# The two MLP products of a decoder layer by seven quarter products in place of eight

## Chip, cores and metric

The kernel runs on one core of a Trainium2 chip. The metric is the device time of one execution in microseconds, the median of the runs.

## What is computed

One decoder layer on 1024 prompt tokens and 64 sample tokens (8 batches of 8), 1088 in all, of width 1024. An attention sub-layer (differential heads and sparse-attention heads, both with caches) is followed by an output projection and a dense MLP with four times the width. Everything is fp32. The part that matters here:

```python
mix = jnp.concatenate([o_diff, o_nsa], axis=-1) @ w_out          # 1088 x 1024 @ 1024 x 1024
x = x + rms_norm(mix, g_post_mix)
hm = rms_norm(x, g_pre_mlp)
ff = jnp.square(jax.nn.relu(hm @ w_up)) @ w_down                 # w_up 1024 x 4096, w_down 4096 x 1024
x = x + rms_norm(ff, g_post_mlp)
```

## The kernel before

An fp32 operand is kept as two tiles of TensorE's fast fp32 type, `hi` (a rounded copy, made on ScalarE) and `lo` (what is left, a subtraction on VectorE or GpSimd). Each product is three products: hi by hi, lo by hi, hi by lo. With weights as the stationary 128x128 operand, the moving operand is a stretch of tokens.

The instructions of a stage are written for each engine in a program order; the scheduler of the framework then orders each engine's queue by when operands are ready in its own model, with the program order as priority, and puts in the semaphores. Buffers of a pool are reused in turn. Pools are stacked in SBUF from the left (and, where `side="right"`, from the right) in the order in which they are opened; a tile of a new pool waits for the accesses to those earlier tiles that lay at its addresses (`reuse_waits="tile"`).

Around the change there are three stages. `stage_diff` is the last attention stage; its pools on the left are `xa` (split input, 70 KB a partition), `b` and `sg`, `sm` (constants, masks, small tiles), `kv2`, `pp2` and others. `phase_out` projects its result (`mixT`, in DRAM) by `w_out`, nine token tiles of two products each (L1267), with `front` (load and split of a tile), `prod`, and `post` (norm, residual stored to `x1d`, second norm, transposes into the split tile `xt`). Its 16 split weight tiles (`w2`) are the first pool on the left, over `xa`.

`phase_mlp` goes over 16 groups of 256 hidden columns and three token chunks (`CHUNKS`, 384, 384, 320). `up` (L1335) makes two blocks of 24 matmuls, `r` and `h` are relu and square, split into hi and lo on ScalarE, GpSimd and VectorE (L1339 to L1343), and stay in SBUF. `down` of the step before (L1355) then makes eight blocks of six matmuls, and VectorE adds each to the accumulator `acc` in SBUF (L1361). The weights of the next group are loaded and split meanwhile (L1231, L133, L162). A chunk needs only its own token tiles, so `up` of the first chunk starts while `phase_out` still works on the last tiles, and `finish` (transposes, norm, residual, store; L1387 to L1404) of a chunk goes beside the matmuls of the next.

## Time and profile before

| what | value |
|---|---|
| median of three runs (lowest, highest) | 1871.66 us (1869.86, 1874.77) |
| span of the profiled execution | 1873.6 us |
| TensorE busy | 1783.9 us, 95% |
| VectorE, ScalarE, GpSimd busy | 961.5, 720.6, 530.2 us |

For the profiled execution only its span is listed, from the first to the last instruction; it lies 1.9 us above the median and within the three runs. A row of a busy-time view gives the line of the kernel, the engine (PE is TensorE's matmuls, PEld its weight loads, DVE VectorE, ACT ScalarE, POOL GpSimd), output and inputs, and the shape. The ends of matmuls are modelled, so pace is read from starts or from long runs of them.

### The profile page before, as it was taken

Reading aid. Unit: us, or ns where it says so; the run is one execution under the profiler, and the core shown is the slowest. Engines: PE = TensorE matmul, PEld = TensorE weight load, DVE = VectorE, ACT = ScalarE, POOL = GpSimd, SP = SyncE. Lnnn points to the kernel's source line nnn. Section 1 sums busy time; section 2 is a strip of 40 time slices with the busy share of each in tenths; the row PEclk is TensorE's granted clock in tenths of the full one; section 3 lists DMA queues with packets and bytes.
Section 4 is the critical chain, followed back from the end, with each engine's and each line's share of the span. In section 5 each row is a group of like instructions: output and inputs, shape, how many; then the busy total and the mean of one; then the engine's idle time right before and its main releaser. Section 6 shows DMA issues by size and latency. Waiting matters only on the chain. (4 is left out here: it accounts for less than half of the span.)

```text
span 1873.6 us, 31247 instructions
## 1 busy us (share of the span) xinstructions
PE 1783.9 (95%) x11379; PEld 1566.2 (84%) x11379; DVE 961.5 (51%) x2519; ACT 720.6 (38%) x1987; POOL 530.2 (28%) x749
## 2 busy tenths in 40 slices
PE   6788999999999999999979999999999999999996
PEld 6777776676657788778868799999999999999996
DVE  4357767667754666666564553333333333333336
ACT  4254446556652455555463342222222222222212
POOL 1133325333321111111151023333333333333313
PEclk8899899999999999999989999999999999999998
DMA  8531000022102524324263331111111111111104
GB/s 169 119 86 44 17 12 21 6 80 52 28 8 58 155 72 125 100 66 124 68 201 106 124 119 46 43 43 45 42 45 45 46 46 46 45 46 46 46 1 169
DMA packets 186533, 129.38 MB, mean 69 GB/s; under 512 B 30115, under 2 KB 177419, under 8 KB 186379
## 3 DMA queue, kind: packets, MB, share of 16 engines
q1 hardware_dynamic: 185082, 125.11, 23.5%
q10 hardware_dynamic: 1296, 2.27, 0.5%
q8 instruction: 90, 1.47, 0.3%
q14 instruction: 65, 0.52, 0.1%
HBM read 102.56 MB, written 24.78 MB: 68 GB/s over the span
## 5 line engine op out<-in xcount | busy, mean ns | idle before, releaser
L1355 PE MATMUL Dn<-h,w 128*128 128x384 f32 (+1 forms) x2304 | 388.6, 327 | 2.1 <-DVE w L1401 2.1
L1335 PE MATMUL U<-xt,w 128*128 128x384 f32 (+1 forms) x2304 | 388.5, 326 | 0.2 <-ACT xt L133 0.2
L1355 PEld LDWEIGHTS Dn<-h,w 128*128 128x128 f32 x2304 | 381.8, 188 | 2.3 <-ACT w L1395 2.3
L1335 PEld LDWEIGHTS U<-xt,w 128*128 128x128 f32 x2304 | 380.4, 188 | 0.6 <-ACT xt L133 0.4
L331 PE MATMUL M<-w,xt 128*128 128x384 f32 (+4 forms) x1584 | 294.6, 331 | 13.5 <-ACT nat L133 13.2
L1361 DVE TENSOR_TENSOR acc<-Dn,acc 128x384 f32<-128x384 f32 (+1 forms) x360 | 191.8, 535 | 204.9 <-PE Dn L1355 203.5
L331 PEld LDWEIGHTS M<-w,xt 128*128 128x128 f32 (+1 forms) x1584 | 245.1, 191 | 28.9 <-ACT nat L133 14.7
L162 POOL TENSOR_TENSOR w<-raw,w 128x512 fp32r<-128x512 f32 x128 | 170.8, 1346 | 177.4 <-ACT w L133 177.4
L421 ACT ACTIVATE p<-S,nm 128x512 f32<-128x512 f32 (+3 forms) x288 | 160.1, 562 | 103.6 <-DVE nm L416 57.1
L133 ACT ACTIVATE w<-raw 128x512 fp32r<-128x512 f32 (+1 forms) x160 | 96.6, 609 | 241.8 <-PE U L1335 166.0
L1343 DVE TENSOR_TENSOR h<-r,h 128x384 fp32r<-128x384 f32 (+1 forms) x96 | 52.0, 542 | 261.8 <-POOL r L1342 261.8
L412 DVE TENSOR_REDUCE nm<-S 128x1 f32<-128x512 f32 (+3 forms) x288 | 148.0, 527 | 58.1 <-PE S L411 37.0
L1339 ACT ACTIVATE r<-U 128x384 f32<-128x384 f32 (+1 forms) x96 | 45.4, 473 | 342.3 <-PE U L1335 342.3
L404 PE MATMUL S<-kst,qs 128*128 128x512 f32 (+3 forms) x576 | 163.2, 376 | 9.0 <-ACT p L421 7.9
L1342 POOL TENSOR_TENSOR r<-r 128x384 f32<-128x384 f32 (+1 forms) x96 | 77.3, 805 | 328.6 <-ACT h L1341 328.6
L475 POOL TENSOR_SCALAR p<-p,coef 128x640 f32<-128x640 f32 (+7 forms) x128 | 92.8, 738 | 146.4 <-DVE coef L472 79.6
L404 PEld LDWEIGHTS S<-kst,qs 128*128 128x128 f32 x576 | 94.5, 196 | 21.7 <-ACT p L421 11.1
L169 POOL TENSOR_TENSOR rs_r<-rs_t,mhalf 128x1 f32<-128x1 f32 (+1 forms) x63 | 36.3, 577 | 249.1 <-DVE rs_t L167 236.0
L1267 PE MATMUL C<-w,mh 128*128 128x512 f32 (+1 forms) x432 | 105.5, 401 | 0.8 <-DVE ctmp L1282 0.8
L351 POOL TENSOR_TENSOR rope<-nat,sin 128x128 f32<-128x128 f32 (+3 forms) x81 | 36.3, 448 | 245.5 <-ACT nat L133 234.4
L1267 PEld LDWEIGHTS C<-w,mh 128*128 128x128 f32 (+1 forms) x432 | 78.4, 184 | 22.3 <-DVE ctmp L1282 1.1
L511 PEld LDWEIGHTS T<-ident,p 128*128 128x128 f32 x528 | 57.1, 141 | 39.3 <-issue 35.6
(265 smaller groups left out, 2395.1 us busy)
## 6 DMA issues: line engine op xcount, KB each, us to landing
kvp<-cache_diff_kv SPq DMA_DIRECT2D x128, 128.0 KB
raw<-w_up SPq DMA_DIRECT2D x64, 256.0 KB
raw<-w_down SPq DMA_DIRECT2D x64, 256.0 KB
raw<-w_in SPq DMA_DIRECT2D x32, 192.0 KB
raw<-w_in SPq DMA_DIRECT2D x40, 128.0 KB
xin<-x_prompt SPq DMA_DIRECT2D x8, 512.0 KB
...
```

Of the source, the lines that this page charges most:

```text
L133: self.nc.scalar.activation(out, in_, AF.Copy, scale=scale)
L162: (nc.vector if self.lo_dve else nc.gpsimd).tensor_sub(lo, raw, f32(hi))
L331: nc.tensor.matmul(ps[1][:m, :n], self.xt[c][:, a, k, c0:c0 + m], ws[k][:, b, :n], start=i == 0, stop=i == len(ops) - 1)
L404: nc.tensor.matmul(S[:, a * P - lo:b * P - lo], qs[:, ps, j, :], kst[hf][:, kc, a * P - lo:b * P - lo], start=ps == 0, stop=ps == 1 and no ...
L412: nc.vector.reduce_max(nm[:, n:n + 1], S[:, a * P - lo:b * P - lo], axis=AX.X, negate=True)
L421: nc.scalar.activation(p[:, a * P:b * P], tiles[n][:, a * P - lo:b * P - lo], AF.Exp, bias=nm[:, 0:1], accum_out=sums[:, n:n + 1])
L475: nc.gpsimd.tensor_scalar(v, v, coef[:, sw + 1, j:j + 1], 0.0, op0=OP.mult, op1=OP.add)
L1267: nc.tensor.matmul(ps[:m], mhs[t][:, a, k, :m], ws[n][k][:, b], start=cnt == 0, stop=cnt == 3 * KC - 1)
L1335: nc.tensor.matmul(U[:, :n], ups[f][k // 4][:, a, k % 4, :], self.xt[c][:, b, k, :], start=cnt == 0, stop=cnt == 3 * KC - 1)
L1342: nc.gpsimd.tensor_mul(r[:, :n], r[:, :n], r[:, :n])
L1355: nc.tensor.matmul(O_[:, :n], dns[dm // 2][:, a, f, (dm % 2) * P:(dm % 2 + 1) * P], hs[f][:, b, :n], start=cnt == 0, stop=cnt == 5)
L1361: nc.vector.tensor_add(acc[c][:, dm], O_[:, :n], acc[c][:, dm])
```

## The change

Both MLP products are cut into 2x2 quarters of the matrices, and each set of eight quarter products is replaced by seven products of sums of quarters (Strassen's scheme in Winograd's form, one level). `left` and `right` make the sums of the weight's and of the token side's quarters, in place, and split each of the seven (`split2`). The tokens are cut into two halves of 544 (`HT`): even and odd tiles, each with half of the sample tokens; a matmul has 272 columns (`QT`).

The MLP becomes two stages. `phase_up` holds all seven factors of the token side in SBUF (`xc`, made by `x_factor` from `xf`, 12 of the 14 pieces after `phase_out`), goes over 16 pairs of hidden blocks, makes the seven factors of the next pair's weights meanwhile, combines the products out of four two-bank accumulators, and stores relu squared to `hT` in DRAM. `phase_down` goes over eight groups of 512 hidden rows, loads weights and `hT` rows, makes seven factors of each two steps ahead (`factor`), and adds every product to one of seven accumulators; in the last group the accumulators are folded into the four quarters (`FOLD`), and `finish` follows for ten token tiles. The pools are stacked anew: `xca` and `ur` now lie to the left of `w2`, `xcb` and `us` take the place of `w2`, `cc` and `cl`, and `sp` takes the place of `xf` on the right.

```diff
+HT = TOK // 2
+QT = HT // 2
+UORD = (0, 5, 1, 6, 4, 3, 2)
+DORD = (0, 6, 4, 5, 1, 3, 2)
+FOLD = {0: ((5, 0), (1, 0)), 4: ((2, 4), (4, 6)), 5: ((6, 5), (3, 6), (2, 5), (4, 5))}
 GELU_C = 2.0 * math.sqrt(2.0 / math.pi)
...
+        self.hT = scratch("hT", [FF, TOK])
...
+        ws = []
+        for k in range(KC):
+            raw = self.rp.tile([P, 4, 256], F32, name="ur", bufs=4).rearrange("p a n -> p (a n)")
+            nc.sync.dma_start(raw, w_out[k * P:(k + 1) * P])
+            w = self.wp.tile([P, 2, D], FR, name="w")
+            for n in range(2):
+                c = slice(n * 512, n * 512 + 512)
+                self.act_copy(w[:, 0, c], raw[:, c])
+                nc.gpsimd.tensor_sub(w[:, 1, c], raw[:, c], f32(w[:, 0, c]))
+            ws.append(w)
...
-            self.transpose_to_xt(tmp, t, self.psT)
+            for hf in range(2):
+                T = self.psT.tile([P, 4, P], F32, name="T", tag="T")
+                for k in range(4):
+                    kk = hf * 4 + k
+                    nc.tensor.transpose(T[:, k, :m], tmp[:m, kk * P:(kk + 1) * P], self.ident[:m, :m])
+                ks = slice(hf * 4, hf * 4 + 4)
+                if t == NT:
+                    for h in range(2):
+                        self.act_copy(self.xf[:, ks, h, HT - 32:HT], T[:, :, h * 32:h * 32 + 32])
+                else:
+                    self.act_copy(self.xf[:, ks, t % 2, t // 2 * P:t // 2 * P + P], T[:, :, :])
...
+            if t == 5:
+                self.x_factor(0, 0)
+                self.x_factor(5, 0)
...
+    def split2(self, w, src, lo):
+        self.act_copy(w[:, 0], src)
+        lo.tensor_sub(w[:, 1], src, f32(w[:, 0]))
+    def right(self, q, i, w, add, lo, first):
+        b11, b12, b21, b22 = q
+        if i == first:
+            add.tensor_sub(b12, b22, b12)
+            add.tensor_add(b11, b11, b12)
+        if i == 4:
+            add.tensor_sub(b12, b22, b11)
+        if i == 3:
+            add.tensor_sub(b21, b21, b11)
+        self.split2(w, {0: b11, 6: b12, 4: b12, 5: b11, 1: b21, 3: b21, 2: b22}[i], lo)
+    def left(self, q, i, w, add, lo, s2=None):
+        a11, a12, a21, a22 = q
+        if i == (6 if s2 is None else 5):
+            add.tensor_sub(a11, a11, a21)
+            add.tensor_add(a21, a21, a22)
+        t = a11 if s2 is None else s2
+        if i == 5:
+            add.tensor_sub(t, a22, a11)
+        if i == 2:
+            add.tensor_sub(a12, a12, t)
+        self.split2(w, {0: a11, 6: a11, 4: a21, 5: t, 1: a12, 3: a22, 2: a12}[i], lo)
+    def x_factor(self, i, p):
+        c = slice(p * QT, (p + 1) * QT)
+        q = [self.xf[:, k * 4:k * 4 + 4, t, c] for k, t in ((0, 0), (0, 1), (1, 0), (1, 1))]
+        self.right(q, i, self.xc[i][:, :, :, c], self.nc.vector, self.nc.gpsimd if i in (1, 6, 2) else self.nc.vector, 5)
+    def phase_up(self, wp, tp, psU, close):
+        nc, A, rp = self.nc, self.A, self.rp
+        w_up = A["w_up"][0]
+        NJ = FF // 256
+        raws, W, S2 = {}, {}, {}
+        def load(j):
+            raws[j] = []
+            for kh in range(2):
+                r = rp.tile([P, 4, 256], F32, name="ur", bufs=4)
+                nc.sync.dma_start(r, w_up[kh * 512:kh * 512 + 512, j * 256:j * 256 + 256]
+                                  .rearrange("(k p) c -> p k c", p=P))
+                raws[j].append(r)
+        def factor(j, i):
+            if j == NJ:
+                return
+            r0, r1 = raws[j]
+            q = (r0[:, :, 0:P], r1[:, :, 0:P], r0[:, :, P:256], r1[:, :, P:256])
+            W[j, i] = w = wp.tile([P, 2, 4, P], FR, name="us", bufs=8)
+            if i == 5:
+                S2[j] = wp.tile([P, 4, P], F32, name="s2", bufs=2)
+            self.left(q, i, w, nc.vector, nc.vector if i in (0, 5) else nc.gpsimd, S2.get(j, 0))
+        def mm(ps, j, i, start, pq):
+            w, x = W[j, i], self.xc[i]
+            for p in pq:
                 cnt = 0
                 for a, b in ((0, 0), (1, 0), (0, 1)):
...
+                    for k in range(4):
+                        nc.tensor.matmul(ps[:, p, :QT], w[:, a, k, :], x[:, b, k, p * QT:(p + 1) * QT],
+                                         start=start and cnt == 0, stop=cnt == 11, skip_group_check=True)
                         cnt += 1
...
+        def products(j, pq, nxt):
+            s = slice(pq[0], pq[-1] + 1)
+            n = len(pq)
+            def ptile(x):
+                if pq[0] == 0:
+                    self.ups[x] = psU.tile([P, 2, 512], F32, name=f"U{x}", tag=f"U{x}")
+                t = self.ups[x]
+                return t, t[:, s, :QT]
+            def stile(x, bufs=2):
+                return self.sp.tile([P, 2, QT], F32, name=x, bufs=bufs)[:, :n]
+            def store(f, t, c, eng):
+                h = stile("uh", 4)
+                if eng is None:
+                    nc.scalar.activation(h, c, AF.Relu)
+                    nc.scalar.activation(h, h, AF.Square)
+                else:
+                    eng.scalar_tensor_tensor(h, c, 0.0, c, op0=OP.max, op1=OP.mult)
+                r = (2 * j + f) * P
+                nc.sync.dma_start(self.hT[r:r + P, t * HT + pq[0] * QT:t * HT + (pq[-1] + 1) * QT],
+                                  h.rearrange("p a n -> p (a n)"))
+            a, av = ptile("a")
+            mm(a, j, 0, True, pq)
+            s1 = stile("s1")
+            self.act_copy(s1, av)
+            nxt(0)
+            b, bv = ptile("b")
+            mm(b, j, 5, True, pq)
+            u2 = stile("u2")
+            nc.vector.tensor_add(u2, bv, s1)
+            mm(a, j, 1, False, pq)
+            store(0, 0, av, None)
+            nxt(5)
+            mm(b, j, 6, False, pq)
+            u3 = stile("u3")
+            nc.vector.tensor_add(u3, bv, s1)
+            nxt(1)
+            c, cv = ptile("c")
+            mm(c, j, 4, True, pq)
+            c22 = stile("c22", 1)
+            nc.vector.tensor_add(c22, cv, u3)
+            store(1, 1, c22, None)
+            nxt(6)
+            d, dv = ptile("d")
+            mm(d, j, 3, True, pq)
+            nc.vector.tensor_add(u3, dv, u3)
+            store(1, 0, u3, nc.vector)
+            nxt(4)
+            mm(c, j, 2, False, pq)
+            nc.vector.tensor_add(u2, cv, u2)
+            store(0, 1, u2, nc.vector)
+            nxt(3)
+            nxt(2)
+        self.ups = {}
+        load(0)
+        load(1)
+        for i in UORD:
+            if i in (0, 5):
+                factor(0, i)
+                self.x_factor(i, 1)
+            else:
+                self.x_factor(i, 0)
+                factor(0, i)
+                self.x_factor(i, 1)
+        close()
+        for j in range(NJ):
+            if j + 2 < NJ:
+                load(j + 2)
+            if j == 0:
+                products(0, (0,), lambda i: None)
+                products(0, (1,), lambda i: factor(1, i))
+            else:
+                products(j, (0, 1), lambda i: factor(j + 1, i))
+    def phase_down(self, ap, rp, fp, psD):
+        nc, A = self.nc, self.A
+        w_dn = A["w_down"][0]
+        acc = {i: ap.tile([P, 4, HT], F32, name=f"acc{i}") for i in DORD}
+        gp = ap.tile([P, D], F32, name="gpm")
+        nc.scalar.dma_start(gp, A["g_post_mlp"].to_broadcast([P, D]))
+        NG = FF // 512
+        raws, F = {}, {}
+        def load(g):
+            rows = slice(g * 512, g * 512 + 512)
+            ws, hs = [], []
+            for e in range(2):
+                w = rp.tile([P, 2, D], F32, name="dw", bufs=4)
+                nc.sync.dma_start(w, w_dn[rows].rearrange("(q e p) c -> e p q c", e=2, p=P)[e])
+                h = rp.tile([P, 2, TOK], F32, name="dh", bufs=4)
+                nc.sync.dma_start(h, self.hT[rows].rearrange("(q e p) c -> e p q c", e=2, p=P)[e])
+                ws.append(w)
                 hs.append(h)
...
+            raws[g] = ((ws[0][:, :, 0:512], ws[1][:, :, 0:512], ws[0][:, :, 512:], ws[1][:, :, 512:]),
+                       (hs[0][:, :, 0:HT], hs[0][:, :, HT:], hs[1][:, :, 0:HT], hs[1][:, :, HT:]))
+        def factor(g, i):
+            if i == 0 and g + 1 < NG:
+                load(g + 1)
+            wq, hq = raws[g]
+            w = fp.tile([P, 2, 2, 512], FR, name="wf", bufs=3)
+            self.left(wq, i, w, nc.gpsimd, nc.gpsimd)
+            h = fp.tile([P, 2, 2, HT], FR, name="hf", bufs=3)
+            self.right(hq, i, h, nc.vector, nc.vector, 6)
+            F[g, i] = (w, h)
+        def product(g, i, db):
+            w, h = F[g, i]
+            ps = psD.tile([P, 2, 512], F32, name="Dn", tag="Dn")
+            for p in range(2):
                 cnt = 0
                 for a, b in ((0, 0), (1, 0), (0, 1)):
...
+                    for q in range(2):
+                        nc.tensor.matmul(ps[:, p, :QT], w[:, a, q, db * P:(db + 1) * P],
+                                         h[:, b, q, p * QT:(p + 1) * QT], start=cnt == 0, stop=cnt == 5)
                         cnt += 1
...
+            d = acc[i][:, db].rearrange("p (a n) -> p a n", a=2)
+            if g == 0:
+                nc.vector.tensor_copy(d, ps[:, :, :QT])
+            else:
+                nc.vector.tensor_add(d, ps[:, :, :QT], d)
+        steps = [(g, i) for g in range(NG) for i in DORD]
+        load(0)
+        for n in range(2):
+            factor(*steps[n])
+        first = list(range(0, NT, 2)) + [NT]
+        for n, (g, i) in enumerate(steps):
+            if n + 2 < len(steps):
+                factor(*steps[n + 2])
+            for db in range(4):
+                product(g, i, db)
+                if n == len(steps) - 1:
+                    self.finish(rp, psD, gp, first[db], (acc[1], acc[3]))
+            if g == NG - 1:
+                for x, y in FOLD.get(i, ()):
+                    for db in range(4):
+                        e = nc.gpsimd if db % 2 else nc.vector
+                        e.tensor_add(acc[x][:, db], acc[x][:, db], acc[y][:, db])
+        self.finish(rp, psD, gp, first[4], (acc[1], acc[3]))
+        for t in list(range(1, NT, 2)) + [NT + 1]:
+            self.finish(rp, psD, gp, t, (acc[2], acc[4]))
+    def finish(self, rp, psD, gp, t, acc):
         nc, A = self.nc, self.A
...
+        m, c0, r0 = (32, HT - 32, SEQ + 32 * (t - NT)) if t >= NT else (P, t // 2 * P, t * P)
+        x1 = rp.tile([P, 2, 512], F32, name="dw", bufs=4)
+        nc.sync.dma_start(x1[:m], self.x1d[r0:r0 + m].rearrange("p (a n) -> p a n", a=2))
+        tmp = rp.tile([P, 2, 512], F32, name="dh", bufs=4)
+        ss = self.fs.tile([P, 1], F32, name="fss", bufs=2)
+        N = psD.tile([P, 2, 512], F32, name="Dn", tag="Dn")
         for hf in range(2):
...
             for i in range(4):
...
+                nc.tensor.transpose(N[:m, hf, i * P:(i + 1) * P], acc[hf][:, i, c0:c0 + m], self.ident)
+        nc.scalar.activation(tmp[:m], N[:m], AF.Square, accum_out=ss[:m])
+        r = self.rstd(self.fs, ss[:m], D, m)
+        nc.vector.scalar_tensor_tensor(tmp[:m], N[:m], r[:m], gp[:m].rearrange("p (a n) -> p a n", a=2),
+                                       op0=OP.mult, op1=OP.mult)
+        nc.gpsimd.tensor_add(tmp[:m], tmp[:m], x1[:m])
+        if t >= NT:
+            dst = A["o_y_s"].rearrange("b s d -> (b s) d")[r0 - SEQ:r0 - SEQ + m]
+        else:
+            dst = A["o_y_p"][0, r0:r0 + m]
+        nc.sync.dma_start(dst, tmp[:m].rearrange("p a n -> p (a n)"))
...
+            with self.pool("xca") as xca, self.pool("ur", 4) as self.rp:
+                self.xc = {i: xca.tile([P, 2, 4, HT], FR, name=f"xc{i}") for i in (0, 5)}
+                right = ExitStack()
+                self.xf = right.enter_context(self.pool("xf", side="right")).tile([P, KC, 2, HT], F32, name="xf")
+                with self.pool("w2", 8) as self.wp, self.pool("cc") as cp, self.pool("cl") as cl, \
+                        self.pool("psC", 3, psum=True) as self.psC, self.pool("psT2", 2, psum=True) as self.psT:
+                with self.pool("xcb") as xcb, self.pool("us") as wp, self.pool("psU", psum=True) as psU:
+                    self.xc.update({i: xcb.tile([P, 2, 4, HT], FR, name=f"xc{i}") for i in (1, 2, 3, 4, 6)})
+                    def close():
+                        right.close()
+                        self.sp = right.enter_context(self.pool("sp", side="right"))
+                    self.phase_up(wp, xcb, psU, close)
+                right.close()
+            with self.pool("acc") as ap, self.pool("rd") as rp, self.pool("fd") as fp, self.pool("fs") as self.fs, \
+                    self.pool("psDn", 4, psum=True) as psD:
+                self.phase_down(ap, rp, fp, psD)
```

## Rows read from the trace of the kernel before

**Rows 1.** The page: busy us, share of the span and instructions of each engine.
```profile
PE 1783.9 (95%) x11379; PEld 1566.2 (84%) x11379; DVE 961.5 (51%) x2519; ACT 720.6 (38%) x1987; POOL 530.2 (28%) x749
```

**Rows 2.** Stretches: span, busy of PE, PEld, DVE, ACT, POOL, granted clock, DMA share, GB/s.
```profile
1058.88:1873.60 814.72, 798.48 (x4828) 789.61 (x4826) 304.26 (x572) 188.72 (x381) 244.08 (x232) 0.99 0.18 55
973.20:992.00 18.80, 18.80 (x89) 15.52 (x89) 5.15 (x12) 8.25 (x20) 8.11 (x8) 0.93 0.32 100
...
1112.00:1837.00 725.00, 725.00 (x4415) 724.95 (x4414) 246.69 (x470) 157.29 (x308) 223.63 (x209) 1.00 0.14 42
1837.00:1873.60 36.60, 21.08 (x137) 20.57 (x135) 25.21 (x50) 7.37 (x24) 12.94 (x14) 0.81 0.56 197
```

**Rows 3.** Groups of TensorE's matmuls by shape: count, busy us, mean ns of one.
```profile
L1335 PE MATMUL U<-xt,w 128*128 128x384 f32 x1536 | 272.1, 334 | 0.0
...
L1335 PE MATMUL U<-xt,w 128*128 128x320 f32 x768 | 116.4, 309 | 0.2 <-ACT xt L133 0.2
...
L331 PE MATMUL M<-w,xt 128*128 128x256 f32 x480 | 74.8, 302 | 11.5 <-ACT nat L133 11.5
```

**Rows 4.** Timeline of TensorE, long runs of one shape: start, us, count at the end.
```profile
179.35 3.32 PE L331 MATMUL M<-w,xt 128*128 128x280 f32 x24
...
414.76 3.08 PE L331 MATMUL M<-w,xt 128*128 128x256 f32 x24
...
1382.58 8.51 PE L1335 MATMUL U<-xt,w 128*128 128x384 f32 x48
...
1399.25 7.19 PE L1335 MATMUL U<-xt,w 128*128 128x320 f32 x48
...
1843.87 2.78 PE L1394 MATMUL Dn<-ident,acc 128*128 128x128 f32 x24
```

**Rows 5.** Timeline of VectorE and GpSimd where instructions of both overlap: start, us.
```profile
1104.10 1.28 DVE L1287 SCALAR_TENSOR_TENSOR ctmp<-cx,rs_r,gpre 64x1024 f32<-64x1024 f32 x1 [0.72 <-POOL rs_r L169]
1104.28 1.79 POOL L1342 TENSOR_TENSOR r<-r 128x384 f32<-128x384 f32 x1 [0.21 <-ACT h L1341]
...
1107.30 0.83 POOL L1342 TENSOR_TENSOR r<-r 128x384 f32<-128x384 f32 x1 [1.24 <-ACT h L1341]
...
1381.73 1.30 POOL L162 TENSOR_TENSOR w<-raw,w 128x512 fp32r<-128x512 f32 x1 [0.45 <-ACT w L133]
1381.90 0.49 DVE L1361 TENSOR_TENSOR acc<-Dn,acc 128x320 f32<-128x320 f32 x1 [0.39 <-PE Dn L1355]
...
1867.82 1.25 POOL L1402 TENSOR_TENSOR w<-w,raw 64x512 f32<-64x512 f32 x1 [0.91 <-issue]
1868.38 1.24 DVE L1402 TENSOR_TENSOR w<-w,raw 64x512 f32<-64x512 f32 x1
```

**Rows 6.** Groups by shape on VectorE, ScalarE and GpSimd from 1000 us on.
```profile
L1361 DVE TENSOR_TENSOR acc<-Dn,acc 128x384 f32<-128x384 f32 x240 | 133.3, 557 | 137.4 <-PE Dn L1355 136.0
...
L1361 DVE TENSOR_TENSOR acc<-Dn,acc 128x320 f32<-128x320 f32 x120 | 58.5, 490 | 67.5 <-PE Dn L1355 67.5
...
L162 DVE TENSOR_TENSOR w<-raw,w 128x512 fp32r<-128x512 f32 x16 | 10.7, 696 | 6.0 <-ACT w L133 5.9
...
L1257 DVE TENSOR_TENSOR mh<-mx,mh 128x1024 fp32r<-128x1024 f32 x5 | 6.1, 1218 | 4.5 <-ACT mh L133 4.5
...
L133 ACT ACTIVATE mh<-mx 128x1024 fp32r<-128x1024 f32 x5 | 5.3, 1052 | 1.1 <-PE C L1267 1.1
...
L162 POOL TENSOR_TENSOR w<-raw,w 128x512 fp32r<-128x512 f32 x112 | 148.0, 1331 | 169.8 <-ACT w L133 169.8
...
L169 POOL TENSOR_TENSOR rs_r<-rs_t,mhalf 128x1 f32<-128x1 f32 x23 | 13.6, 592 | 110.5 <-DVE rs_t L167 110.3
```

**Rows 7.** Timeline at the end of phase_out, and the densest stretch of transfers.
```profile
1087.81 5.75 PE L1267 MATMUL C<-w,mh 128*64 128x512 f32 x24
...
1106.43 3.78 PE L1335 MATMUL U<-xt,w 128*128 128x320 f32 x24 [0.22 <-ACT xt L133]
...
1855.00:1860.00 5.00, 5.00 (x42) 4.92 (x40) 3.15 (x8) 1.58 (x5) 0.96 (x1) 1.00 1.03 388
```

More of the change, by code (lines that the diff above doesn't have):

```diff
@@ L1332, in up @@
                 cnt = 0
                 for a, b in ((0, 0), (1, 0), (0, 1)):
-                    for k in range(KC):
-                        nc.tensor.matmul(U[:, :n], ups[f][k // 4][:, a, k % 4, :], self.xt[c][:, b, k, :],
-                                         start=cnt == 0, stop=cnt == 3 * KC - 1)
+                    for k in range(4):
+                        nc.tensor.matmul(ps[:, p, :QT], w[:, a, k, :], x[:, b, k, p * QT:(p + 1) * QT],
+                                         start=start and cnt == 0, stop=cnt == 11, skip_group_check=True)
@@ L1352, in down @@
                 cnt = 0
                 for a, b in ((0, 0), (1, 0), (0, 1)):
-                    for f in range(2):
-                        nc.tensor.matmul(O_[:, :n], dns[dm // 2][:, a, f, (dm % 2) * P:(dm % 2 + 1) * P],
-                                         hs[f][:, b, :n], start=cnt == 0, stop=cnt == 5)
+                    for q in range(2):
+                        nc.tensor.matmul(ps[:, p, :QT], w[:, a, q, db * P:(db + 1) * P],
+                                         h[:, b, q, p * QT:(p + 1) * QT], start=cnt == 0, stop=cnt == 5)
@@ L1357, in down @@
                         cnt += 1
-                if gr == 0:
-                    nc.vector.tensor_copy(acc[c][:, dm], O_[:, :n])
-                else:
-                    nc.vector.tensor_add(acc[c][:, dm], O_[:, :n], acc[c][:, dm])
-        steps = [(gr, c) for gr in range(NG) for c in range(3)]
-        prev = None
-        for gr, c in steps:
-            if c == 0 and gr + 1 < NG:
-                W[gr + 1] = load(gr + 1)
-                self.lo_dve = False
-            hs = up(gr, c)
-            if prev:
-                down(*prev)
-                if prev[0] == NG - 1:
-                    self.finish_chunk(dp, psD, acc, gp, prev[1])
-            prev = (gr, c, hs)
```

87 lines of the change are left out of this document (1 added, 86 removed).

## The prediction

> **What bounds the kernel now.** First the page [rows 1]: TensorE is busy 95% of the span, the others half or less. Then the busy times by stretch [rows 2]: from 1112 to 1837 us, the MLP proper, TensorE is busy 725.00 of 725.00 us at a granted clock of 1.00, VectorE a third, GpSimd 31%. From 1058.88 us (the end of `phase_out`) to the end TensorE stands still for only 814.72 - 798.48 = 16.2 us, nearly all of it in the last 36.6 us. So the MLP is worth what its matmuls cost, every join is covered by other matmuls, and whatever leaves TensorE idle is lost in full.
>
> **TensorE's share of the change.** Before: 3072 matmuls of 384 and 1536 of 320 columns (up [rows 3], and as many in down). Pace from long runs, less the last one's mean duration: (8.51 - 0.334)/47 = 174 ns and (7.19 - 0.309)/47 = 146.4 ns [rows 3, 4]. That is 534.5 + 224.9 = 759.4 us. After: up 16 x 7 x 24 and down 8 x 7 x 48, 5376 of 272 columns. This width does not occur. The line through 320 and 384 gives 125.7 ns; the runs of 256 and 280 columns, (3.08 - 0.302)/23 = 120.8 and (3.32 - 0.30)/23 = 131.3 ns [rows 3, 4], give 127.8. I take 126 (same kind of dense stream): 677.4 us, **-82**; with 127.8 it is -72.
>
> Does the weight load hold up a matmul of 126 ns? PEld is busy 724.95 of 725.00 us [rows 2], but the 256-column runs load 128x128 weights for each matmul at 120.8 ns and the transposes reach (2.78 - 0.272)/23, some 109 ns [rows 3, 4]. So it does not, in my view. The Trainium skill (Perfetto Trace Analysis, Identifying the Most-Contended Engine) says to judge TensorE by the busy share of its weight loads and not by its matmuls. By that the loads would be the bound already; it is the fourth rival below.
>
> **The price list.** PSUM to SBUF adds are 490 and 557 ns for 320 and 384 columns [rows 6], so 0.72 us for 544. VectorE with two SBUF operands: 0.70 us for 512, 1.22 for 1024 [rows 6], so 1.29 for 1088 and 0.74 for 544. GpSimd: 1.33 us for 512 [rows 6]; for 1024 twice that is 2.66, less some fixed part 2.5; for 1088 2.65, for 544 1.41. ScalarE: 1.05 us for 1024.
>
> VectorE and GpSimd are not independent. GpSimd's 384-wide product takes 0.83 us alone, and 1.79 when it starts 0.18 us after a VectorE instruction with two SBUF operands; a VectorE add of 512 takes 1.24 instead of 0.70 and ends 0.55 after the GpSimd add in its way. An add with one operand in PSUM runs through such an overlap at its usual 0.49 [rows 5, 6]. So these times add up when both have work. The Trainium skill (SBUF — State Buffer, Who interferes with whom) gives the rule: VectorE's second SBUF operand and GpSimd go through one exclusive port, and the later one waits. The trace agrees (1.24 and 1.79 us), and without the rule the sum below would be some 40 us lower; it speaks against this change, which moves hundreds of such instructions to these two engines.
>
> **Up, steady state.** A pair of blocks is 168 matmuls, 21.2 us. Port work: GpSimd 5 x 1.33, VectorE (4 sums, 2 lows) x 0.70 and 2 squares x 0.74, 12.3 us. VectorE in all 9.3, ScalarE below 8. The accumulators have one buffer each, but 24 matmuls (3 us) stand between a product and the next into the same one, and the read takes 0.72. Cost nothing; if VectorE came 2 us late, it would show at once.
>
> **Start of phase_out, +8.** Today `w2` lies over `xa`, free early; products of `phase_out` fill the last attention head's waits, PE 18.80 of 18.80 us busy [rows 2]. With `xca` and `ur` (51 KB) to its left, `w2` spans some 51 to 115 KB: its tiles from the third or fourth on lie over `b`, `sg` and `kv2`, in use to the last head. Their splits, 10 x 1.33 = 13.3 us on GpSimd, move behind it. Between 0 and 15; I take 8.
>
> **Start of up, +32.** Today the last product of `phase_out` ends at 1087.81 + 5.75 = 1093.56, and up goes on beside the last tile's norm, 12.9 us to its first use at 1106.43 [rows 7]. Afterwards five of seven `xc` lie over `w2`, `cc` and `cl`, so their factors wait for that last product, call it T. Then come on VectorE 12 x 1.29 + 6 x 0.70, on GpSimd 6 x 2.65 + 5 x 1.33: 42 us through one port. `sp` lies over `xf`, so even the first copy `s1` waits for the last `x_factor`. Before it TensorE can do four of seven products of the first pair; after it 72 matmuls are left, 9 us. The pair ends at T + 51 where its work is 21: 30 lost, 2 more for the granted clock, which falls when TensorE stands still (0.81 in the last stretch [rows 2]). From below: if VectorE did not hold the port, GpSimd alone is 22.5, and 10 are lost. From above: if the port work starts with the last tile's norm done, 42.
>
> **Up to down, +20.** `dw` lies over `xc` tiles that the last product reads, so nothing of `w_down` is loaded before. A group is 2.1 MB of weights and 2.2 of `hT`; at the 388 GB/s that the trace reaches [rows 7] 11 us, its first half 5.6. Then split: 1.05 + 2.5 + 1.29; the first product starts at about 10.5 and lasts 6. The second factor needs the second half: three GpSimd and three VectorE instructions, 11.4 us from 11 on, so 6 more idle. With 3 for the clock: 20; 13 if `hT` comes ahead, 32 at half the rate. The store of `hT` and its loads are elsewhere 4.3 MB in 42 us, 100 GB/s, and cost nothing.
>
> **Down, steady state, +10.** A group is 336 matmuls, 42.3 us. GpSimd: 11 x 2.5 = 27.5. VectorE: 11 x 1.29 and 28 x 0.72 = 34.4. Through the port 41.7. GpSimd is busy 65% of the time; a VectorE instruction that meets it waits on average half of 2.5, so 11 x 0.65 x 1.25 = 9, VectorE 43.4, just above TensorE. The four two-bank buffers let TensorE run about three blocks ahead. 1.2 us a group, 10; bounds 0, and 48 if every one of the 11 waits 1.25.
>
> **The end, +24.** In the last group the port has 7 x 2.5 + 7 x 1.29 of factors left, 32 folds (16 x 1.41 + 16 x 0.74), and GpSimd does ten residual adds and powers (2.5 + 0.59 [rows 6]): 92 us, 4 more to the last store, against 42.3 + 80 x 0.109 = 51 of TensorE. 45 idle, and the folds stand ahead of the last factor in program order, so the last product waits too. Today 16 are idle there: +29, less what VectorE does while GpSimd waits: 24. GpSimd alone, 71 us, gives +8; 30 from above.
>
> **Sum.** -82 + 8 + 32 + 20 + 10 + 24 = +12. The sum is against the span of 1873.6; the median is 1.9 lower: 1871.7 + 12 = **1884 us**, slightly slower. All bounds low: -82 + 0 + 10 + 13 + 0 + 8 = -51; all high: -72 + 15 + 42 + 32 + 48 + 30 = +95.
>
> **Rivals.** (1) Faster: the port costs less than it adds up to, because the two engines' waits fall into each other's gaps at the start of up. If GpSimd alone sets that join (10 in place of 32) and the end (8 in place of 24), the sum is -26; with down at 0 and the other joins as low as they go, -51. 1835 on average. It decides from the point at which the start of up costs less than 14. For it: VectorE and GpSimd are idle half the time today; against it: [rows 5]. (2) Down becomes bound by VectorE behind GpSimd: +48 in place of 10, 1922. For it: 43.4 against 42.3 leaves no reserve; against: the buffers. (3) The joins hide one another so that gain and loss are equal, 1868 to 1876. (4) The weight loads set the pace: 759.4/4608 = 165 ns each, 5376 of them 886 us, +126 in place of -82, 2092. For it: PEld without a gap; against: [rows 4].
>
> **Chances.** About 0.3% (6 us) is what a measurement of this kernel can tell from no change. My forecast, slower by 6 to 40 us: 0.44; (2) 0.09; (4) 0.02; (3) 0.13; (1) 0.32. So faster 0.32, same 0.13, slower 0.55. The forecast's own range is 1878 to 1912. The range that leaves out (4), half of (2) and the better fifth of (1) is 1836 to 1924.
>
> **What would show it.** Pace: runs of 272 columns at 126 ns; above 140 it is the weight loads. Start: first C products after 980 us. A hole of about 30 us between the last C and the second pair of up, with VectorE's and GpSimd's two-operand instructions end to end and stretched. A hole of 10 us and one of 6 at the start of down. Down groups of 43 to 44 us. At the end 40 us with GpSimd busy and TensorE idle. I am wrong if those holes are short because factors were made earlier than I think, or if the stretched instructions do not occur.

## Result and the profile after

The changed kernel takes 1913.58 us (median of four runs, 1910.13 to 1917.81) against 1872.16 for the kernel before (four runs): ratio 1.0225, 95% interval 1.0204 to 1.0246. It is slower, as forecast, but by 41 us where 12 were forecast. That lies inside the wide range of the prediction (1836 to 1924) and 2 us above the forecast's own (1878 to 1912).

The page of the kernel after, busy times, beside [rows 1]:

```profile
PE 1725.2 (90%) x12155; PEld 1497.5 (78%) x12155; DVE 1233.4 (65%) x2539; ACT 806.3 (42%) x1976; POOL 746.3 (39%) x733
```

TensorE has 59 us less to do and the span is 37 us longer (1910.7): about 96 us more in which it stands still. The stretches of the kernel after, columns as in [rows 2]; in order: the hole ahead of the first C, start of up, up, start of down with its first group, six further groups, the last group with `finish`, and a part of up:

```profile
972.10:981.54 9.44, 0.02 (x1) 0.00 (x0) 0.02 (x1) 4.84 (x9) 9.44 (x9) 0.50 0.79 243
1090.84:1152.10 61.26, 30.93 (x184) 28.92 (x183) 47.43 (x43) 27.89 (x46) 38.80 (x18) 0.67 0.12 35
1152.10:1468.42 316.32, 316.32 (x2522) 316.10 (x2520) 129.78 (x189) 107.27 (x173) 99.95 (x71) 1.00 0.30 99
1468.42:1533.90 65.48, 48.34 (x338) 46.28 (x337) 54.99 (x44) 18.96 (x19) 46.17 (x16) 0.90 0.55 204
1533.90:1809.40 275.50, 259.15 (x2016) 253.65 (x2017) 263.60 (x234) 88.06 (x85) 194.38 (x66) 1.00 0.23 83
1809.40:1910.70 101.30, 61.41 (x416) 57.54 (x416) 74.20 (x74) 21.49 (x30) 79.81 (x44) 0.81 0.23 78
1180.00:1400.00 220.00, 220.00 (x1755) 220.00 (x1754) 91.71 (x134) 77.27 (x126) 74.17 (x54) 1.00 0.30 101
```

Only up runs without a gap: 220.00/1755 is 125.4 ns a matmul. In down's six groups VectorE is busy 263.60 of 275.50 us and TensorE stands still for 16. Five of the six groups take 46.5 us each from first matmul to first matmul, where 336 x 125.4 ns are 42.1; the sixth takes 43.0. The instructions of these six, by shape (count, busy us, mean ns, idle time before):

```profile
L1519 PE MATMUL Dn<-hf,wf 128*128 128x272 f32 x2016 | 259.2, 289 | 16.4 <-DVE acc L1526 15.7 <-DVE acc L1524 0.2
...
L1331 POOL TENSOR_TENSOR wf<-dw,wf 128x1024 fp32r<-128x1024 f32 x42 | 118.5, 2821 | 79.3 <-ACT wf L139 79.3
L1526 DVE TENSOR_TENSOR acc<-Dn,acc 128x544 f32<-128x544 f32 x165 | 111.9, 713 | 11.6 <-PE Dn L1519 11.5
L1331 DVE TENSOR_TENSOR hf<-dh,hf 128x1088 fp32r<-128x1088 f32 x42 | 94.7, 2254 | 0.0
```

VectorE's subtraction of 1088 columns takes 2254 ns in place of 1.28 us, its addition from PSUM 713, as forecast. The timeline of the worst step of a group, VectorE, then GpSimd, then TensorE:

```profile
1662.42 3.48 DVE L1338 TENSOR_TENSOR dh<-dh 128x1088 f32<-128x1088 f32 x1
1665.82 0.71 DVE L1526 TENSOR_TENSOR acc<-Dn,acc 128x544 f32<-128x544 f32 x1
1666.45 2.83 DVE L1339 TENSOR_TENSOR dh<-dh 128x1088 f32<-128x1088 f32 x1
...
1661.43 3.32 POOL L1350 TENSOR_TENSOR dw<-dw 128x1024 f32<-128x1024 f32 x1
1664.83 3.31 POOL L1351 TENSOR_TENSOR dw<-dw 128x1024 f32<-128x1024 f32 x1
...
1666.59 1.76 PE L1519 MATMUL Dn<-hf,wf 128*128 128x272 f32 x12 [1.30 <-DVE acc L1526]
1669.97 3.30 PE L1519 MATMUL Dn<-hf,wf 128*128 128x272 f32 x24 [1.63 <-DVE acc L1526]
```

The two engines take turns: each VectorE sum ends 1.1 us after the GpSimd sum that it waited for, each GpSimd sum waits for the VectorE one. The addition that frees a PSUM buffer stands behind them, and TensorE waits.

The start of up shows the same on VectorE's timeline; the last row is a sum of the same shape, and GpSimd has no instruction beside it:

```profile
1101.05 3.58 DVE L1343 TENSOR_TENSOR xf<-xf 128x1088 f32<-128x1088 f32 x1 [2.40 <-POOL xc L1331]
1104.56 3.57 DVE L1338 TENSOR_TENSOR xf<-xf 128x1088 f32<-128x1088 f32 x1
...
1118.57 1.28 DVE L1339 TENSOR_TENSOR xf<-xf 128x1088 f32<-128x1088 f32 x1
```

### The profile page after: what moved, and what is told of

The parts are those of the page before. It is cut to its first block, busy times and chain, and to the rows that moved or that the text cites. A ratio compares the mean times of both kernels' runs of the same rounds, so it can differ in the third digit from the quotient of the medians.

```text
span 1910.7 us, 32861 instructions
## 1 busy us (share of the span) xinstructions
PE 1725.2 (90%) x12155; PEld 1497.5 (78%) x12155; DVE 1233.4 (65%) x2539; ACT 806.3 (42%) x1976; POOL 746.3 (39%) x733
## 4 chain that ended last, share of the span: by engine, by line
PE 71%; DVE 13%; issue 3%; DMA 3%; POOL 2%; ACT 2%; SPq 0%; POOLq 0%; ACTq 0%; DVEq 0%
PE M L337 11%; PE Dn L1519 10%; PE C L1272 5%; PE S L410 5%; PE Ua L1395 5%; PE Ub L1395 5%; PE Uc L1395 5%; PE o L502 5%; PE T L517 4%; PE Ud L1395 3%; DVE hf L1331 2%; DVE acc L1526 2%; PE o L614 2%; PE S L1095 1%; DVE dh L1338 1%
## 5 line engine op out<-in xcount | busy, mean ns | idle before, releaser
L1519 PE MATMUL Dn<-hf,wf 128*128 128x272 f32 x2688 | 358.0, 294 | 47.3 <-DVE acc L1526 29.7
L1519 PEld LDWEIGHTS Dn<-hf,wf 128*128 128x128 f32 x2688 | 348.1, 193 | 56.8 <-DVE acc L1526 33.9
L337 PE MATMUL M<-w,xt 128*128 128x384 f32 (+4 forms) x1584 | 293.0, 330 | 13.1 <-ACT nat L139 12.8
L1331 POOL TENSOR_TENSOR wf<-dw,wf 128x1024 fp32r<-128x1024 f32 x56 | 157.7, 2818 | 119.6 <-ACT wf L139 119.6
L1331 POOL TENSOR_TENSOR us<-ur,us 128x512 fp32r<-128x512 f32 x80 | 118.3, 1481 | 211.8 <-ACT us L139 189.2
L1526 DVE TENSOR_TENSOR acc<-Dn,acc 128x544 f32<-128x544 f32 x196 | 132.9, 712 | 15.1 <-PE Dn L1519 14.9
L1331 DVE TENSOR_TENSOR hf<-dh,hf 128x1088 fp32r<-128x1088 f32 x56 | 127.1, 2270 | 8.0 <-ACT hf L139 8.0
L1395 PE MATMUL Ua<-xc,us 128*128 128x272 f32 x768 | 107.1, 292 | 9.9 <-DVE us L1331 8.9
L1395 PE MATMUL Ub<-xc,us 128*128 128x272 f32 x768 | 103.5, 290 | 9.7 <-ACT us L139 9.7
L1395 PE MATMUL Uc<-xc,us 128*128 128x272 f32 x768 | 108.4, 290 | 3.5 <-POOL us L1331 3.2
L1395 PEld LDWEIGHTS Ua<-xc,us 128*128 128x128 f32 x768 | 102.0, 193 | 10.4 <-DVE us L1331 9.2
```

The lines of the kernel that those rows point to most:

```text
L337: nc.tensor.matmul(ps[1][:m, :n], self.xt[c][:, a, k, c0:c0 + m], ws[k][:, b, :n], start=i == 0, stop=i == len(ops) - 1)
L1331: lo.tensor_sub(w[:, 1], src, f32(w[:, 0]))
L1395: nc.tensor.matmul(ps[:, p, :QT], w[:, a, k, :], x[:, b, k, p * QT:(p + 1) * QT], start=start and cnt == 0, stop=cnt == 11, skip_group_che ...
L1519: nc.tensor.matmul(ps[:, p, :QT], w[:, a, q, db * P:(db + 1) * P], h[:, b, q, p * QT:(p + 1) * QT], start=cnt == 0, stop=cnt == 5)
L1526: nc.vector.tensor_add(d, ps[:, :, :QT], d)
```

## The experiments

The theory: TensorE's 85 us are saved, and the instructions that make the quarter sums and low parts give them back, because VectorE's with two SBUF operands and GpSimd's exclude each other (below, "the port"). Rivals: VectorE's own load, waits for addresses at the joins, transfers, the order of the steps. Times are medians; the ratio is to the kernel before, run on the same chip.

**e1, start of up on VectorE alone.**

```diff
-self.nc.gpsimd if i in (1, 6, 2) else self.nc.vector, 5)
+self.nc.vector, 5)
-nc.vector if i in (0, 5) else nc.gpsimd, S2.get(j, 0))
+nc.vector if j == 0 or i in (0, 5) else nc.gpsimd, S2.get(j, 0))
```

> At the start of up every two-operand instruction goes to VectorE: 6 low parts of the token factors and 5 of the first pair's weight factors leave GpSimd. Theory (their times add up, so a GpSimd instruction costs its own longer time): the hole shrinks by 6 x (2.40 - 1.28) + 5 x (1.33 - 0.70), 10 us; the second pair starts at about 1142 us in place of 1152, time 1904. Rival (the engines work side by side, the hole is VectorE's load): VectorE gets 6 x 1.28 + 5 x 0.70, 11 us more, time 1925. Second rival (ScalarE's copies or the norm of the last tile set the hole): no change, 1911 to 1916.

Measured: 1905.83, ratio 1.0178 (1.0152 to 1.0203); the second pair starts at 1142.1. VectorE's groups by shape there:

```profile
L1331 DVE TENSOR_TENSOR xc<-xf,xc 128x1088 fp32r<-128x1088 f32 x12 | 14.9, 1276 | 0.0
L1331 DVE TENSOR_TENSOR us<-ur,us 128x512 fp32r<-128x512 f32 x7 | 4.5, 680 | 0.3 <-ACT us L139 0.3
```

Eleven instructions more on VectorE, and the second pair starts 10 us earlier, as the port theory said; the rival had the other sign. The time fell by 8 us.

**e2, buffers of down where up's tiles come free first.**

```diff
-with self.pool("acc") as ap, self.pool("rd") as rp, self.pool("fd") as fp, ...
+with self.pool("rd") as rp, self.pool("fd") as fp, self.pool("acc") as ap, ...
-for i in (1, 2, 3, 4, 6)})
+for i in (1, 6, 4, 3, 2)})
-nc.sync.dma_start(self.hT[r:r + P,
+(nc.scalar if j == NJ - 1 and (f, t) != (0, 1) else nc.sync).dma_start(self.hT[r:r + P,
```

> The buffers of down lie so that the first group's weights and hT rows fall on tiles that the last pair of up reads first, and three of the last four stores of hT go by ScalarE's queue. Theory (the join is the wait for those addresses): the loads start some 10 us before the end of up, the holes of 9.2 and 2.4 us shrink to some 4 in all, the first group's first steps are not late, time 1900. Rival (the loads wait for hT to be stored, or the first group is slow because of the split work on GpSimd and VectorE): the first hole stays above 7 us or its time comes back later in the group, 1910 to 1914.

Measured: 1912.14, ratio 1.0203 (1.0178 to 1.0228). The first hole falls from 9.2 to 1.6 us, but the first group takes 60.9 us in place of 56.3: the rival. The addresses were one of two waits in a row; behind them stand the factors, again with VectorE held up (its timeline):

```profile
1475.71 2.74 DVE L1420 SCALAR_TENSOR_TENSOR uh<-u 128x544 f32<-128x544 f32 x1
1478.37 3.47 DVE L1331 TENSOR_TENSOR hf<-dh,hf 128x1088 fp32r<-128x1088 f32 x1
```

**e3, no GpSimd work in down's groups.**

```diff
-self.left(wq, i, w, nc.gpsimd, nc.gpsimd)
+a11, a12, a21, a22 = wq
+t = {0: a11, 6: a11, 4: a21, 5: a11, 1: a12, 3: a22, 2: a12}[i]
+self.act_copy(w[:, 0], t)
+self.act_copy(w[:, 1], t)
```

This kernel leaves out the sums of `w_down`'s quarters, and its low parts are copies, so it does not compute the layer; it is there for its time alone.

> Leaves out the sums of w_down's quarters and makes both tiles of a weight factor by ScalarE copies, so that GpSimd has no work in down but folds and finish. Theory (GpSimd's 11 instructions hold VectorE's two-operand ones up): those fall from 2.2 to 3.4 us to 1.28, VectorE to 34 us a group, the group from 46.5 to 42.1 us; with eight groups and a lighter join and end 35 to 50 us less, 1863 to 1878. Rival (VectorE's additions of PSUM, their order or the number of PSUM buffers set the pace): VectorE's two-operand times fall but the group stays at 45 to 46.5 us, 1905 to 1913. Second rival (ScalarE, now at 14 + 7 copies a group, becomes late): the group is longer, over 1913.

Measured: 1872.61, ratio 0.9999 (0.9988 to 1.0011): 41 us less than the changed kernel. Six groups of it, columns as above, and VectorE's subtraction:

```profile
1531.00:1781.90 250.90, 250.90 (x2019) 250.90 (x2018) 193.25 (x234) 126.34 (x126) 0.00 (x0) 1.00 0.27 92
```

```profile
L1331 DVE TENSOR_TENSOR hf<-dh,hf 128x1088 fp32r<-128x1088 f32 x42 | 53.9, 1282 | 0.0
```

TensorE has no gap and a group takes 41.8 us, 4.7 less than the changed kernel's 46.5. PSUM buffers and the additions alone are not the bound.

**e4, e8: the end.** e4 puts all folds on VectorE (`e = nc.vector`); e8 is

```diff
-tmp = rp.tile([P, 2, 512], F32, name="dh", bufs=4)
+tmp = self.fs.tile([P, 2, 512], F32, name="ft", bufs=6)
-nc.gpsimd.tensor_add(tmp[:m], tmp[:m], x1[:m])
+(nc.vector if t % 4 > 1 or t == NT else nc.gpsimd).tensor_add(tmp[:m], tmp[:m], x1[:m])
```

> All 32 folds of the accumulators on VectorE (0.74 us each alone), none on GpSimd (1.41). Theory (folds add up on both engines): 16 x (1.41 - 0.74), 11 us less of that work, of which 6 to 10 show, time 1904 to 1908. Rival (VectorE, which also empties PSUM, is what the end waits for): 16 x 0.74, 12 us more on it, time 1920 to 1925.

> Five of the ten residual adds of finish go to VectorE, and the result tiles get six buffers of their own. Theory (after the last product GpSimd is the bound: 10 x 2.35 + 10 x 0.55, 29 of 35 us): GpSimd 17, VectorE 10 x 1.24 + 5 x 1.28 = 19, and 6 to 10 us less, time 1904 to 1908. Rival (the chain of transposes, square, power and store, and its PSUM buffers): 0 to 2 us.

Measured: e4 1913.63, ratio 1.0221 (1.0195 to 1.0247); e8 1911.08, ratio 1.0212 (1.0185 to 1.0239). Neither time can be told from the changed kernel's, though in the profiles the last group with `finish` takes 97.6 and 95.8 us in place of 101.3. e4 followed neither theory nor rival: VectorE is busy 28.4 us with all 32 folds, and was busy 24.7 with 16 of them beside GpSimd's. e8 came out near its rival, 2 us less.

**e5, the order 0, 1, 6, 4, 5, 3, 2** in `DORD`.

> Down takes its products in the order 0, 1, 6, 4, 5, 3, 2: the second factor of a group then needs no sums, and the heaviest one (three instructions on VectorE, three on GpSimd) comes a step later. Theory A (the sum of the two engines' times over a whole group is too long): the group stays at 46 to 46.5 us, only the start of down gains 4 to 6, time 1908. Theory B (only the peak is too long for the four PSUM buffers, and the peak now falls into slack): the group falls to 43 to 44.5, time 1888 to 1898.

Measured: 1910.64, ratio 1.0202 (1.0173 to 1.0232); five of the groups take 45.7 us where the changed kernel's take 46.5. That is theory A for the most part: the sum over a group is too long, and the peak's share is 0.8 us. The gain of 4 to 6 us at the start of down did not come: from the end of up to the second group it is 64.8 us in place of 65.6.

**e6, the token side's sums in up.** `hT` is stored as seven combinations; the core of it:

```diff
+nc.vector.tensor_sub(h12, h22, h12)
+put(6, h12)
+nc.vector.tensor_add(o5, h11, h12)
+put(5, o5)
+nc.vector.tensor_sub(o4, h22, o5)
+put(4, o4)
+nc.vector.tensor_sub(o3, h21, o5)
+put(3, o3)
...
-self.right(hq, i, h, nc.vector, nc.vector, 6)
+self.split2(h, hq[i], nc.vector)
```

> The four sums of the token side's quarters are made in up, on VectorE, and hT holds seven combinations in place of four quarters (1.75 times the bytes). Theory (GpSimd and VectorE share one port; up has 21.1 - 12.3 us of it free in a pair, down has none): pairs stay at 21.1 us; in down VectorE has 7 x 1.28 + 28 x 0.71 = 28.9 us and at most 11 waits of 1.2, so the group is TensorE's 42; 8 x 4.4 = 35 us less, 2 to 4 more at the join, time 1872 to 1880. Rival (the sums only move the load): pairs grow to 22 us and more, 16 x 1 back, time over 1890. Second rival (transfers, 6 MB in a group, 143 GB/s): the group waits for dh.

Measured: 1886.68, ratio 1.0075 (1.0047 to 1.0103). Pairs stay at 21.1 us, groups fall to 42.4; six of them:

```profile
1537.90:1792.10 254.20, 254.20 (x2018) 254.20 (x2017) 222.29 (x212) 86.69 (x84) 182.20 (x67) 1.00 0.37 121
```

Down's gain came as forecast. The join went wrong: the hole before the first product grew from 9.2 to 18.1 us. The hole as a stretch, and VectorE's timeline in it:

```profile
1475.10:1493.20 18.10, 0.00 (x1) 0.00 (x0) 4.25 (x6) 2.19 (x3) 7.02 (x3) 0.58 0.97 352
```

```profile
1478.89 0.72 DVE L1470 TENSOR_TENSOR uh<-uh 128x544 f32<-128x544 f32 x1
1493.20 3.69 DVE L1331 TENSOR_TENSOR hf<-dh,hf 128x1088 fp32r<-128x1088 f32 x3 [13.60 <-ACT hf L139]
```

VectorE has made the last pair's four sums by 1479.6 us and then stands idle for 13.6, while the DMA engines are 97% busy: by these rows the join waits for transfers, which the seven combinations have made longer (the second rival, but at the join alone). No run tried that apart; in e10, where the loads start earlier, the hole before the first product is 1.1 us.

**e7, `xca` and `ur` at the right end of SBUF** (`side="right"` on both pools).

> xca and ur go to the right end of SBUF, so that w2 lies over xa again, as in the kernel before. Theory (the split of w_out waits for the last head's tiles): GpSimd's 16 low parts come before 970 us, the hole of 9.4 us before the first C shrinks to 1 or 2, time 1904 to 1907. Rival (the hole is the last head's own latency, mixT stored and loaded again): no change, 1911 to 1915.

Measured: 1923.65, ratio 1.0276 (1.0245 to 1.0308), slower than either expected. The splits do come early (from 942.9 us) and the hole is gone, but the last attention matmuls end at 988.8 in place of 972.1. VectorE and GpSimd there, first beside a run of six GpSimd instructions, then beside a run of eight:

```profile
947.35 6.81 DVE L422 TENSOR_TENSOR nm<-nm 128x1 f32<-128x1 f32 x1
...
956.80 0.97 DVE L422 TENSOR_TENSOR nm<-nm 128x1 f32<-128x1 f32 x1
...
946.74 7.41 POOL L1246 TENSOR_TENSOR w<-ur,w 128x512 fp32r<-128x512 f32 x6
...
956.48 10.85 POOL L1246 TENSOR_TENSOR w<-ur,w 128x512 fp32r<-128x512 f32 x8
```

An instruction on one column, 0.15 us in the changed kernel, took 6.81: it waited out six GpSimd instructions that followed each other without a pause (their run ends at 954.15 us, it at 954.16), and the softmax behind it waited too. That is not the rule: the run of eight let six of VectorE's instructions in between, one of the same line among them, each 0.5 to 1.1 us late. What made the difference is not shown.

**e9, no GpSimd in down, its work on VectorE** (`self.left(wq, i, w, nc.vector, nc.vector)`).

> In down VectorE makes all sums and low parts; GpSimd has only folds and finish. VectorE is then 22 x 1.28 + 28 x 0.71 = 48.1 us a group, with no waits for a port. Theory (GpSimd's 11 instructions hold the port): the group goes from 46.5 to 48 us and no further, so that 25.7 us of work on GpSimd spared 1.6 us a group; the join and the end, where the port alone decides, gain some of it back; time 1912 to 1926. Rival (GpSimd relieves VectorE by its own share, something else adds the 4.4 us a group): VectorE's 48.1 plus that 4.4, groups of 52, over 1950.

Measured: 1896.29, ratio 1.0127 (1.0111 to 1.0142): 17 us faster than with GpSimd's help, where at best a gain of 2 was expected. Six groups, VectorE's additions as a group, and a row of its timeline:

```profile
1531.50:1796.70 265.20, 257.04 (x2016) 253.93 (x2017) 260.62 (x300) 87.45 (x84) 0.00 (x0) 1.00 0.24 87
```

```profile
L1526 DVE TENSOR_TENSOR acc<-Dn,acc 128x544 f32<-128x544 f32 x140 | 96.7, 729 | 1.4 <-PE Dn L1519 1.4
```

```profile
1588.19 2.62 DVE L1526 TENSOR_TENSOR acc<-Dn,acc 128x544 f32<-128x544 f32 x4
```

A group takes 44.3 us, below the 48.1 that I had added up, because instructions in a row overlap: four additions took 2.62 us, (2.62 - 0.73)/3 = 0.63 each.

**e10, e11, e12, combined.** e10 is e1, e5, e6, e2's order of pools (with the order 1, 2, 6, 4, 3 and the early stores of the last pair on ScalarE's queue), e4, and e8's residual adds. e11 adds e9 and takes e4 back. e12 is e11 with `nc.vector` for the low parts of `w_out`.

> Together: the token side's sums in up, the start of up on VectorE alone, the order 0, 1, 6, 4, 5, 3, 2, down's buffers over tiles that up's last pair reads first (the stores of that pair that are ready early go by ScalarE's queue), all folds and half of the residual adds on VectorE. From the run with the sums in up, 1886.7: start of up 9 less, the hole of 18 us between up and down 12 to 15 less, the end 0 to 5 less: 1858 to 1866, faster than the kernel before. Rival (the hole comes back as late steps of the first group, as in the run with early buffers): 1872 to 1878, no gain over the kernel before.

> As the combined kernel (1879.0), but in down VectorE makes all sums and low parts of the weights too, and half of the folds go back to GpSimd. Theory (the join's 17 us of late steps are VectorE's last sums of up, 2.7 us each behind GpSimd in place of 0.74): those sums take 0.75 us again, the holes of 11.7 and 5.5 us shrink to 4 to 6 in all, groups stay at 42.4 us (28 x 0.63 + 18 x 1.2 = 39 us for VectorE), time 1864 to 1870, faster than the kernel before. Rival (VectorE alone is too slow for the first two factors, and the last group's folds wait longer): the join gains less than 5 us and the end loses that, 1876 to 1882.

> As the run before it, and the 16 low parts of w_out on VectorE (0.70 us each, VectorE idle there) in place of GpSimd (1.23). Theory (the hole of 9.4 to 9.8 us before the first C is the load of the first mx, queued behind loads of w_out that wait for GpSimd's splits): the splits end 8 us earlier, the first mx is issued 2 to 3 us earlier, the hole is 6 to 8 us, 2 to 4 us less in all. Rival (VectorE's last attention steps are delayed by the splits, as they were on GpSimd when these came earlier): the last attention matmul comes later by as much or more, 0 to 6 us more.

Measured: e10 1878.98, ratio 1.0038 (1.0023 to 1.0052); e11 1870.05, 0.9994 (0.9983 to 1.0004); e12 1873.23, 1.0011 (0.9998 to 1.0024). e10 followed its rival, and came out just above it: holes of 11.7 and 5.5 us in the first group. The last pair's sums in e10, and in e11 with the first copies out of PSUM:

```profile
1464.12 2.70 DVE L1461 TENSOR_TENSOR uh<-uh 128x544 f32<-128x544 f32 x1
```

```profile
1461.15 0.72 DVE L1461 TENSOR_TENSOR uh<-uh 128x544 f32<-128x544 f32 x1
...
1477.96 2.62 DVE L1539 COPY acc<-Dn 128x544 f32<-128x544 f32 x4
```

So e11 wins by what e10 lost to the port; of its join 4.1 and 6.3 us remain, where 4 to 6 in all were expected. e12 refutes what I thought of the first hole: the splits end earlier, yet the first `mx` goes out at 977.5, behind a store of the last attention tile and two loads of `w_out` in SP's queue; its split starts 7.1 us later (4.9 in the changed kernel), and the hole is 13.1 us.

**e13, e14, e15: what is left.** e13 is e11 with ScalarE copying the first group's products out of PSUM (`self.act_copy(d, ps[:, :, :QT])`); e14 is e11 with

```diff
+DORD = (0, 1, 6, 5, 4, 3, 2)
+FOLD = {0: ((5, 0), (1, 0)), 5: ((6, 5), (3, 6), (2, 5)), 4: ((2, 4), (4, 6))}
-x1 = rp.tile([P, 2, 512], F32, name="dw", bufs=4)
+x1 = rp.tile([P, 2, HT], F32, name="dh", bufs=14)[:, :, :512]
```

and e15 is e13's edit and e14's.

> As e11 (1870.1), but in the first group of down ScalarE copies the products out of PSUM. Theory (the hole of 6.3 us before the second product is four PSUM buffers that wait for VectorE, which makes six factor instructions first): that hole goes, the first group falls from 55.9 to 48 to 50 us, 5 to 8 less, time 1862 to 1865. Rival (the factors themselves are late, the buffers only show it): the first group stays above 54 us, 1868 to 1871.

> As e11, but with the order 0, 1, 6, 5, 4, 3, 2: seven sets of folds in place of eight, and three of them one step earlier; the residual rows are loaded into buffers that are free earlier. Theory (in the last group the folds stand ahead of VectorE's additions from PSUM and TensorE waits): holes of 1.2, 3.0 and 7.2 us before the last two steps shrink to 5 in all, and 2 to 4 us of waits for the residual rows go, time 1861 to 1866. Rival (the end is the sum of VectorE's work and changes only by the set left out, 3 us): 1867 to 1870.

> Both edits of the two runs before. If both theories hold, the savings add up: 1854 to 1860, faster than the kernel before by 0.6 to 0.9%. If neither, 1866 to 1871.

Measured: e13 1878.54, ratio 1.0031 (1.0018 to 1.0045); e14 1861.61, 0.9949 (0.9930 to 0.9968); e15 1869.16, 0.9990 (0.9976 to 1.0005). e13 is slower; ScalarE's timeline says why:

```profile
1485.99 0.34 ACTq L1500 DMA_DIRECT2D gpm<-g_post_mlp  x1
1486.38 2.17 ACT L139 ACTIVATE acc<-Dn 128x544 f32<-128x544 f32 x4 [8.52 <-DMA dh<-hT]
```

The copies stand behind the issue of the `gpm` load, which waits for a transfer; the hole grew to 11.3 us. TensorE goes on 0.7 us after the first copy starts, so PSUM is what it waits for in that hole; the cure was not tried with that load elsewhere.

e14 is the first version that beats both kernels, by 0.5% against the kernel before. Its first group, six groups and end:

```profile
1460.70:1517.30 56.60, 45.13 (x338) 44.72 (x338) 49.50 (x56) 17.43 (x18) 0.00 (x0) 0.91 0.82 302
1517.30:1768.10 250.80, 250.80 (x2017) 250.80 (x2017) 234.93 (x277) 86.69 (x84) 0.00 (x0) 1.00 0.39 127
1768.10:1857.10 89.00, 58.56 (x418) 55.16 (x416) 76.34 (x82) 21.22 (x30) 46.53 (x29) 0.85 0.23 77
```

The end takes 89.0 us where e11's took 96.9: its three edits together; which of them did it was not tried apart. The pair e13 and e15 shows the same gain, 97.7 to 89.7 us at the end, so e15 is e14's gain with e13's loss, and not two savings, as was expected. e14's groups are also 0.6 us shorter (41.8 against 42.4), 3.4 us in six. That is no wait: TensorE has no gap in either, and its matmuls start every 124.4 ns in e14 and e3, every 126.1 in e6, e11 and e15. Why is open, since e15 has e14's order; so a third of e14's 10 us is not shown to come from its edits.

## Why the prediction was right in sign and too low in size

The terms, forecast and found in the profiled execution, whose span rose by 37.1 (a steady group is 46.5 us, its matmuls 42.1, a pair's 21.1, the end's transposes 8.7):

| term | forecast | found | how |
|---|---|---|---|
| pace of 272 columns | -82 | -85 | 5376 x 125.4 ns against 759.4 |
| start of phase_out | +8 | +9 | the hole of 9.4 |
| start of up | +32 | +40 | second pair at 1152.1, - 21.1 - 1090.8 |
| up to down | +20 | +19 | 65.5 - 42.1, less 4.4 of the steady loss (46.5 - 42.1) |
| down, steady | +10 | +27 | 275.5 - 6 x 42.1, and 4.4 |
| the end | +24 | +34 | 101.3 - 42.1 - 8.7 = 50.5, today 16 |

They add up to +44; 7 us come back ahead of `phase_out`, in stages that the change leaves alone. There the 40 matmuls `o<-kvp,dpt` of the last head, which every kernel here has, start at 938.5 us after and 946.0 before, and between 938.6 and 945.1 in the fifteen experiments: executions of one program differ by that much. By the medians the change costs 41.

**The pace** was right, and rival (4) is out. The weight loads are busy 220.00 of 220.00 us and the matmuls still start every 125.4 ns. The rule that I had cited (the Trainium skill, Perfetto Trace Analysis, Identifying the Most-Contended Engine) names the share of the weight loads, beside the share of peak FLOPs, as a sign of how much room TensorE has. As that it agrees with this trace, where up has no gap; that the loads set the pace was my reading, and it does not hold.

**Down, steady** is the term that was most mis-sized. The step that failed is "GpSimd is busy 65% of the time; a VectorE instruction that meets it waits on average half of 2.5, so 11 x 0.65 x 1.25 = 9", and in it the 0.65. The half was right: the wait is (2254 - 1282) ns on each low part and 0.9 to 2.1 us on each sum, 1.17 on average, half of GpSimd's 2.34. But it is not a chance meeting: both engines' instructions come in runs and then alternate, so that all 66 of VectorE's two-operand instructions in the six groups waited (the least 0.3 us), some 13 us a group. That made VectorE busy 263.60 of 275.50 us. e3 shows the price, 4.7 us a group, of which 0.6 may be the faster pace that its matmuls have. It is the case of my upper bound of 48, every one of the 11 waiting, and rival (2), VectorE behind GpSimd as the bound, named the mechanism that I gave 0.09.

**Start of up** was mis-sized by 8: 42, the bound from above, is nearer. The norm of the last tile is not covered by anything (a hole of 7.1 us). The port part was right: it ran from 1097.6 to 1136.8 us, 39 where 42 were forecast, and e1 took away the 10 that it should. Behind it 120 of the pair's 168 matmuls were left, 16 us, where I had 72 and 9.

**Start of phase_out** came out at its size, but not for the reason given. By e12 it is the first `mx` in SP's queue, not GpSimd's splits; by e7 splits that come earlier cost more than the hole. That term was right by luck.

**Up to down** was right in size, and its two parts (loads, then factors) are what e2 and e10 separated.

**The end** was 10 too low. Folds of 0.74 and 1.41 us by the price list took 1.58 and 1.91, side by side (VectorE's and GpSimd's rows in the last group, then the stretch up to the last three products):

```profile
L1544 DVE TENSOR_TENSOR acc<-acc,acc 128x544 f32<-128x544 f32 x16 | 24.7, 1578 | 0.0
```

```profile
L1544 POOL TENSOR_TENSOR acc<-acc,acc 128x544 f32<-128x544 f32 x16 | 30.2, 1914 | 3.1 <-DVE acc L1526 3.1
```

```profile
1809.40:1868.50 59.10, 45.28 (x302) 43.77 (x303) 57.22 (x49) 10.47 (x10) 51.36 (x24) 0.88 0.06 19
```

The sum of 92 us had the folds one after the other, 34 us, so the stretching was in it. It left out VectorE's 28 additions from PSUM, 20 us by the price list, and it took 5 off for overlap. VectorE is busy 57.22 of these 59.10 us, with folds ahead of the additions that TensorE waits for; that this makes up the 10 is read from the rows, not tried. e14 shows that order, number of folds and buffers together are worth 8 us of it.

**The rule of the port** (the Trainium skill, SBUF — State Buffer, Who interferes with whom) was the right one to weigh against this change; e1, e3 and e9 are in line with it. It says that the later one waits. Mostly that was one instruction of the other engine; in one place of e7 it was a whole run.
